# Norm factors from a matmul with ones, and the last up pair in seven products

## The chip, the cores and the metric

The kernel runs on one core of a Trainium2 chip. The metric is device time in microseconds of one launch; the number told for a kernel is the median of its runs. Engines are named as in the profile: PE is TensorE (matmuls; PEld its weight loads), DVE VectorE, ACT ScalarE, POOL GpSimd, SP the queue that issues most transfers.

## The reference

A two-layer encoder trunk over 512 positions with 1024 channels, in float32. Layer 0 mixes tokens with causal pooling and a short gated convolution, layer 1 with gated linear attention in 4 heads. After each mixer comes a gated feed-forward part with a convolution. Every part is preceded by an RMS norm, the attention output is normed per head, and a last norm ends the trunk.

```
def rmsnorm(x, g):
    y = x * rsqrt(mean(x * x, axis=-1) + EPS)
    return y * g

for l in range(2):
    hn = rmsnorm(x, mix_norm[l])
    if l == 0:
        y = concat(pool_mixer(...), sb * causal_dwconv(sc * sx)) @ ab_w_out
    else:
        y = gla_mixer(hn @ gla_w_in, ...) @ gla_w_out     # o * rsqrt(mean(o * o) + EPS) per head
    x = x + y
    u, v = split(rmsnorm(x, ffn_norm[l]) @ w_up[l])
    x = x + (gelu(causal_dwconv(u)) * v) @ w_down[l]
return rmsnorm(x, final_norm)
```

## The kernel before

Channels lie on the 128 partitions, the 512 positions along the free dimension, so x is 8 tiles of 128x512. Each matrix product is made of three matmul passes: both operands are split into a high and a low part (`split`, lines 157 to 159: ACT copies to a rounded type, DVE subtracts), and high by high, high by low and low by high are summed in one PSUM bank (`accumulate`, line 255; one output tile of 128 channels from 1024 takes 24 matmuls with 512 columns). Weights come from memory block by block through SP into three buffers `raw`; ACT makes `hi` (line 214), DVE makes `lo` (line 218).

The norm is applied late: the products are made of x times the gain, and the factor `rs`, one number per position, is multiplied in afterwards. ACT squares x (line 279) and DVE adds the squares into `acc`. `sums` (line 305) adds over the partitions with four matmuls that have `acc` as weights and one column of ones, so that positions lie on partitions (`ss`, 128x4). `rsqrt_small` (lines 282 to 292) takes the square root on ACT, the reciprocal on DVE, and one Newton step in three small DVE operations. `spread_small` (line 297) makes four matmuls with an identity to spread the 128x4 result over all partitions as 128x512 (`bc`), and ACT copies that to `rs` (line 319) or, per attention head, to `ro` (line 902). This happens at seven places with a wide result that the change touches: the first norm (`norm_rows`), the norm of each feed-forward part (`norm_parts`, in `ffn_up`) and the four heads (`out_norm`, `out_scale`). The norm ahead of the attention and the last one use the small form as well.

`ffn_up` makes 22 pairs of u and v tiles per layer. Pairs 1 to 20 use `seven`: u and v and the two halves of channels and positions are combined so that seven quarter products (each 12 matmuls with 256 columns, line 520) do the work of eight. Their weight sums need more transfers and work on ACT and DVE: `s31` is loaded by SP twice side by side and POOL's queue adds to it, the left half and a quarter are loaded, and three high and low parts and two differences are made (lines 471, 478, 483, 489). Pairs 0 and 21 use `plain`: v and u each with 24 matmuls of 512 columns (line 435). In this stage PE, DVE and ACT run in an order written out by hand: every step is entered with a due time by `at(...)`, in units of a product, and the list is sorted by it. The last products p4 and p3 of a pair are placed behind the first ones of the next pair. What follows on a pair (`keep` copies out of PSUM, line 528; the convolution, gelu, the product with v) ends in `ms[j]`, which `split_m` splits into `mh` and `ml` for the down product (`ffn_down`, PSUM tile `dn`). Eight side tiles share memory with the buffers of the seven-product stage: they hold `mh` and `ml` of the last four pairs.

Outside `ffn_up` the order on each engine is set by a scheduler from the program text: functions handed to `after(n, ...)` run n projections later (`tick`). In the attention stage, the four heads' scores, recurrences, outputs (`o`) and norms are so placed between the eight projections `r` (`gate_r`). `out_gate` of a head waits for `sil`, the silu of r, and then makes `y`, `yh` and `yl`. Each engine works through its own queue in order; a PE matmul that waits holds up all matmuls behind it.

Of the kernel before, what the change touches and what calls it, by code (L numbers as in the profile page):

```python
# [7 lines left out]
F32 = mybir.dt.float32  # L8
# [5 lines left out]
P = 128  # L14
# [27 lines left out]
UNIT = 1.364  # L42
PAIR = 7 * UNIT
PLAIN = 8 * UNIT
NORM = 1.6
PE_AT = {"p1": 0, "p2": 1, "p6": 3, "p5": 5, "p7": 6, "p4": 9, "p3": 11}
DOWN_K = (8, 7, 7)
DOWN_AT = (0, 8, 15)

# [14 lines left out]
def trunk_kernel(ctx, tc, xT, cols, w_ab, w_pool, w_abo, w_vg, w_qkr, w_g2, w_go, w_up, w_dn, outT):  # L64
# [11 lines left out]
    def slot(dt=F32, name="s"):  # L76
        return big.tile([P, T], dt, tag="s", name=name)
# [17 lines left out]
    def bank(name="ps"):  # L95
        return ps.tile([P, T], F32, tag="ps", name=name)
# [35 lines left out]
    for k in range(3, KD):  # L132
        x_load(k)

    cp.tile([P, 48], F32, tag="gap", name="gap")
# [4 lines left out]
    sp.tile([P, 72], F32, tag="gap", name="gap", bufs=1)  # L140
    warm_in = sp.tile([P, 1], F32, tag="warm", name="warm_in", bufs=1)
    S.activation(warm_in, ones[:, 0:1], AF.Sqrt)
# [4 lines left out]
    V.memset(eps_t, EPS)  # L147
    ident = cp.tile([P, P], F32, tag="ident", name="ident")
    G.memset(ident, 1.0)
    G.affine_select(ident, ident, [[-1, P]], ALU.is_equal, 0.0, base=0, channel_multiplier=1)  # L150
# [18 lines left out]
    def weight_order():  # L169
        for g in range(2, 4):  # L170
            yield w_ab[g], KD, P
        for j in range(4):
            for b in (8 + j, 12 + j, 4 + j):
                yield w_ab[b], KD, P
        for j in TILE_ORDER:
            yield w_abo[j], KD, P
        for l in range(2):
            for j in range(NF):
                if j in (0, NF - 1):
# [60 lines left out]
    def after(n, fn):  # L240
        pending.append((done[0] + n, fn))
# [40 lines left out]
    def rsqrt_small(dst, ssum, n, width):  # L282
        v = sp.tile([P, n], F32, tag=f"v{n}", name="v")
        V.tensor_scalar(v, ssum, 1.0 / width, EPS, ALU.mult, ALU.add)
        s = sp.tile([P, n], F32, tag=f"s{n}", name="s")
        S.activation(s, ssum, AF.Sqrt, bias=eps_t, scale=1.0 / width)
        y = sp.tile([P, n], F32, tag=f"y{n}", name="y")
        V.reciprocal(y, s)
        t = sp.tile([P, n], F32, tag=f"t{n}", name="t")
        V.tensor_tensor(t, y, v, ALU.mult)  # L290
        V.scalar_tensor_tensor(t, t, -0.5, y, ALU.mult, ALU.mult)
        return s, V.scalar_tensor_tensor(dst, t, 1.5, y, ALU.add, ALU.mult).ins

    def spread_small(y, n):
        b = bank("bc")[:, : n * P]
        for c in range(n):
            PE.matmul(
                b[:, c * P : (c + 1) * P], y[:, c : c + 1].broadcast_to([P, P]), ident, start=True, stop=True
            )
        return b  # L300

    def sums(acc, c0=0, n=NTT):
        b = bank("ss")
        for c in range(n):
            PE.matmul(b[:, c : c + 1], acc[:, (c0 + c) * P : (c0 + c + 1) * P], ones[:, 0:1], start=True, stop=True)
        return b

    def norm_parts(acc, gelu=False):
        y4 = sp.tile([P, NTT], F32, tag="y4", name="y4")
        rs = slot(name="rs")  # L310

        def one():
            s, last = rsqrt_small(y4, sums(acc)[:, :NTT], NTT, D)
            if gelu:
                S.activation(sp.tile([P, 1], F32, tag="warm", name="warm", bufs=1), s[:, 0:1], AF.Gelu)
            return last

        def two():
            S.activation(rs, spread_small(y4, NTT), AF.Copy)

        return y4, rs, one, two

    def norm_rows(acc, first, second):
        y4, rs, one, two = norm_parts(acc)
        after(first, one)
        after(second, two)
        return y4, rs

    def residual(j, o, next_gain, acc):
# [51 lines left out]
        return out  # L381

    def ffn_up(l, acc, mixed):
        _, rs, norm_one, norm_two = norm_parts(acc, True)
        skew = SKEW[l]
        lo_t, hi_t = slice(0, H), slice(H, T)
        k1, k2 = range(HK), range(HK, KD)
# [14 lines left out]
        def at(t, fn):  # L402
            events.append((t, len(events), fn))
# [44 lines left out]
        def seven(j, base):  # L448
# [96 lines left out]
            for name, out, first, ts in (  # L545
                ("p1", "x", True, lo_t), ("p2", "yz", True, lo_t), ("p6", "x", False, lo_t), ("p5", "yz", False, hi_t),
                ("p7", "x", False, lo_t), ("p4", "x", False, lo_t), ("p3", "yz", False, hi_t),
            ):
                at(base + PE_AT[name] * UNIT, lambda a=(name, out, first, ts): product(*a))
# [6 lines left out]
            at(after + 4.5, u_scaled)  # L556
            conv_at(j, after, q)
            at(after + 10.4, lambda: V.tensor_tensor(q["k"], b["yz"], q["k"], ALU.add))
            at(after + 12.3, lambda: V.tensor_tensor(q["a"], q["k"], q["a"], ALU.mult))

        mh, ml = [], []

        def split_m(n):
            for j in range(len(mh), min(len(mh) + n, NF)):
                make = side if j >= NF - NSIDE // 2 else slot
# [5 lines left out]
        at(2.5 * PLAIN / 6, norm_one)  # L571
        at(5.5 * PLAIN / 6 + NORM / 2, norm_two)
        step = PLAIN / 6
        base = PLAIN + NORM
        plain(0, 0.0, [i * step + NORM / 2 * ((i > 2) + (i > 5)) for i in range(6)], base)
        for j in range(1, NF - 1):
            seven(j, base)
            base += PAIR
        block(base - 14.0, base - 6.75, base - 4.35)
        block(base - 9.0, base - 2.7, base - 0.3)  # L580
        last = PLAIN + 2 * UNIT
        plain(NF - 1, base, [i * last / 6 for i in range(6)], base + last - 4.0)
        at(base + 2.0, lambda: open_stage("side"))
        for t in (0.6, 1.3, 2.0, 2.7, 5.7, 8.7, 9.4, 11.0):
            at(base + t, lambda: split_m(1))
        block(base - 3.0, base + 4.6, base + 9.0)
        with tc.manual_schedule(engines={mybir.EngineType.PE, mybir.EngineType.DVE, mybir.EngineType.Activation}):
            for t, _, fn in sorted(events, key=lambda e: e[:2]):
                fn()
# [55 lines left out]

    y_h = [slot(F32R, "yh") for _ in range(8)]
    y_l = [slot(F32R, "yl") for _ in range(8)]
    _, rs = norm_rows(acc, 1, 2)

    def pool_front(g, win, pu):  # L650
        u = slot(name="pu")
# [248 lines left out]
    def out_scale(h, ob, yo):  # L900
        ro = slot(name="ro")
        S.activation(ro, spread_small(yo, NTT), AF.Copy)
        ys = []
        for e in range(2):
            y = slot(name="y")
            V.scalar_tensor_tensor(y, ob[e], col("gnorm", e), ro, ALU.mult, ALU.mult)
            ys.append(y)
        after(1, lambda: out_gate(h, ys))
# [34 lines left out]
    tc.keep_in_program_order(S.activation(ready_in, ones[:, 0:1], AF.Sqrt))  # L943
    mixed = mix_out("go", "ffn1", acc)
    assert not pending

# [120 lines left out]
```

## Time and profile before

| | |
|---|---|
| median of 3 runs | 1045.44 us (1045.11 to 1045.96) |
| the profiled execution | 1045.42 us |
| its span from the first to the last instruction | 1043.7 us |
| busy share PE, PEld, DVE, ACT, POOL | 99, 89, 71, 54, 5% |
| mean granted TensorE clock | 0.997 |

The profile is one execution. A row of the timeline has the start, the duration from the first start to the last end, the engine, the line, the operation, output and inputs, and the count of instructions; in brackets stands the idle time before it and what ended that. Matmuls are pipelined, so the time one costs in a stream is the distance between starts and not its duration. A row of the list of waits has the total, the count and the longest wait. A matmul of plain 32-bit type shows as two records, one of the rounded type as one.

### The profile page before, as it was taken

Reading aid. Unit: us, or ns where it says so; the run is one execution under the profiler, and the core shown is the slowest. Engines: PE = TensorE matmul, PEld = TensorE weight load, DVE = VectorE, ACT = ScalarE, POOL = GpSimd, SP = SyncE. Lnnn points to the kernel's source line nnn. Section 1 sums busy time; section 2 is a strip of 40 time slices with the busy share of each in tenths; the row PEclk is TensorE's granted clock in tenths of the full one; section 3 lists DMA queues with packets and bytes.
Section 4 is the critical chain, followed back from the end, with each engine's and each line's share of the span. In section 5 each row is a group of like instructions: output and inputs, shape, how many; then the busy total and the mean of one; then the engine's idle time right before and its main releaser. Section 6 shows DMA issues by size and latency. Waiting matters only on the chain.

```text
span 1043.7 us, 16375 instructions
## 1 busy us (share of the span) xinstructions
PE 1030.1 (99%) x6614; PEld 929.2 (89%) x6614; DVE 739.9 (71%) x1060; ACT 560.0 (54%) x828; POOL 52.8 (5%) x79
## 2 busy tenths in 40 slices
PE   9999999999999999999999999999999999999996
PEld 7888889999999878889988888889999999988886
DVE  7875669999999874444465555678999999873333
ACT  6432557676667642234773355656766776653321
POOL 0001000110110000010000001000111110000000
PEclk9999999999999999999999999999999999999998
DMA  6436226878875243333232117135887775243312
GB/s 226 137 117 161 65 88 164 199 194 201 195 186 144 82 145 94 99 93 109 82 107 87 49 41 181 41 111 139 200 199 186 190 202 151 82 143 99 105 36 81
DMA packets 53644, 135.94 MB, mean 130 GB/s; under 512 B 4704, under 2 KB 7136, under 8 KB 53568
## 3 DMA queue, kind: packets, MB, share of 16 engines
q1 hardware_dynamic: 41456, 112.74, 34.2%
q0 software_dynamic: 10880, 20.97, 12.7%
q10 hardware_dynamic: 1232, 1.17, 0.4%
q8 instruction: 52, 0.85, 0.3%
q14 instruction: 24, 0.20, 0.1%
HBM read 132.77 MB, written 2.10 MB: 129 GB/s over the span
## 4 chain that ended last, share of the span: by engine, by line
PE 92%; DVE 3%; ACT 2%; DMA 1%; issue 1%; SPq 0%; DVEq 0%; ACTq 0%
PE dn L255 21%; PE stx L520 20%; PE styz L520 15%; PE r L255 4%; PE abo L255 4%; PE go L255 4%; PE q L255 2%; PE k L255 2%; PE pc L255 2%; PE px L255 2%; PE pb L255 2%; PE vg L804 1%; PE vg L802 1%; PE vg L803 1%; PE v L435 1%; PE u L435 1%
## 5 line engine op out<-in xcount | busy, mean ns | idle before, releaser
L214 ACT ACTIVATE hi<-raw 128x1024 fp32r<-128x1024 f32 (+3 forms) x111 | 112.9, 1019 | 164.8 <-PE dn L255 95.8
L218 DVE TENSOR_TENSOR lo<-raw,hi 128x1024 fp32r<-128x1024 f32 (+3 forms) x111 | 130.2, 1173 | 83.8 <-PE dn L255 48.5
L478 DVE TENSOR_TENSOR lo<-raw,hi 128x1024 fp32r<-128x1024 f32 x80 | 97.5, 1219 | 3.4 <-ACT hi L471 3.4
L471 ACT ACTIVATE hi<-raw 128x1024 fp32r<-128x1024 f32 x80 | 84.7, 1059 | 21.9 <-PE styz L520 17.2
L255 PE MATMUL dn<-mh,hi 128*128 128x512 f32 (+1 forms) x374 | 88.9, 377 | 0.5 <-ACT mh L158 0.5
L255 PE MATMUL dn<-mh,lo 128*128 128x512 f32 (+1 forms) x374 | 88.5, 376 | 0.0
L255 PE MATMUL dn<-ml,hi 128*128 128x512 f32 (+1 forms) x374 | 88.1, 376 | 0.0
L458 POOL DMA_DIRECT2D s<-in_w_up x40 | 48.2, 1205 | 670.8 <-DVE raw L489 189.6
L255 PEld LDWEIGHTS dn<-mh,hi 128*128 128x128 f32 x374 | 67.3, 188 | 14.6 <-ACT mh L158 1.9
L255 PEld LDWEIGHTS dn<-mh,lo 128*128 128x128 f32 x374 | 67.5, 188 | 12.9
L255 PEld LDWEIGHTS dn<-ml,hi 128*128 128x128 f32 x374 | 67.4, 188 | 12.8
L351 DVE SCALAR_TENSOR_TENSOR cacc<-u,colt,cacc 128x511 f32<-128x511 f32 x96 | 71.4, 744 | 2.4 <-ACT cacc L348 2.2
L348 ACT ACTIVATE cacc<-u,colt 128x512 f32<-128x512 f32 x48 | 39.2, 817 | 37.4 <-DVE u L543 29.4
L270 ACT ACTIVATE xh<-xall,colt 128x512 fp32r<-128x512 f32 x32 | 22.9, 723 | 58.4 <-DVE xall L330 57.0
L520 PE MATMUL stx<-th,hi 128*128 128x256 f32 x320 | 49.3, 276 | 0.0
L520 PE MATMUL styz<-xh,hi 128*128 128x256 f32 x320 | 49.3, 276 | 0.0
L520 PE MATMUL stx<-th,lo 128*128 128x256 f32 x320 | 49.3, 276 | 0.0
L520 PE MATMUL styz<-xh,lo 128*128 128x256 f32 x320 | 49.3, 276 | 0.0
L520 PE MATMUL styz<-xl,hi 128*128 128x256 f32 x320 | 49.3, 276 | 0.0
L520 PE MATMUL stx<-tl,hi 128*128 128x256 f32 x320 | 49.3, 276 | 0.0
L478 DVE TENSOR_TENSOR lo<-s,hi 128x1024 fp32r<-128x1024 f32 x40 | 48.6, 1216 | 0.0
L471 ACT ACTIVATE hi<-s 128x1024 fp32r<-128x1024 f32 x40 | 42.5, 1062 | 1.2
(279 smaller groups left out, 2304.3 us busy)
## 6 DMA issues: line engine op xcount, KB each, us to landing
raw<-in_w_up SPq DMA_DIRECT2D x48, 512.0 KB, 6.5
s<-in_w_up SPq DMA_DIRECT2D x40, 512.0 KB, 7.1
s<-in_w_up POOLq DMA_DIRECT2D x40, 512.0 KB, 6.5
raw<-in_w_dn SPq DMA_DIRECT2D x32, 448.0 KB, 3.2
raw<-in_w_up SPq DMA_DIRECT2D x40, 256.0 KB, 3.0
raw<-in_w_dn SPq DMA_DIRECT2D x16, 512.0 KB, 3.5
raw<-in_w_qkr SPq DMA_DIRECT2D x16, 512.0 KB, 3.6
raw<-in_w_ab SPq DMA_DIRECT2D x14, 512.0 KB, 3.5
```

The costliest lines, as they stand in the source:

```text
L214: S.activation(parts[0], raw, AF.Copy)
L218: V.tensor_tensor(parts[1], raw, f32(parts[0]), ALU.subtract)
L255: PE.matmul(out, w[:, k, :], a[k], start=first and i == 0 and k == 0, stop=last and i == 2 and k == n - 1)
L270: done = S.activation(xh[k], x[k], AF.Copy, scale=col(gname, k))
L348: S.activation(acc[0], u, AF.Identity, bias=col(bname, j), scale=col(wname, 2 * nj + j))
L351: V.scalar_tensor_tensor(a, u[:, : T - i], col(wname, (2 - i) * nj + j), a, ALU.mult, ALU.add)
L435: PE.matmul(o, w[:, k, :], a[k], start=i == 0 and k == 0, stop=i == 2 and k == KD - 1)
L458: G.dma_start(w["s31"].rearrange("p (a n) -> p a n", a=2), src, accum_op=ALU.add)
L471: S.activation(h, src(), AF.Copy)
L478: V.tensor_tensor(lo, src(), f32(h), ALU.subtract)
L520: PE.matmul(b[out][:, ts], wt[:, ks[k]], a[k], start=first and i == 0 and k == 0, stop=i == 2 and k == HK - 1, skip_group_check=True,)
L802: PE.matmul(o[c][:, :n], xh[kk][:, cs], h[:, k, :], start=kk == 0, stop=False)
```

## The change

1. `norm_wide` replaces the small form at the seven places. It splits `acc` into `nh` (ACT) and `nl` (DVE), sums over partitions with two matmuls whose weights are a 128x128 tile of ones, so that every partition gets the sums 512 wide, takes the inverse root from a table on ACT (`ny`), and makes one Newton step in four wide operations (square on ACT, DVE, ACT, DVE) to `rs`. The first norm makes `nh` and `nl` at once and the rest one projection later; `ffn_up` enters the eight parts by due times; `out_norm` runs all of them in a row, and `out_scale` follows one projection later.
2. In the small form that remains, the root and the reciprocal become one inverse root on ACT.
3. In `ffn_up` the load of the gelu table is an entry of its own, behind the norm; the two waits of 0.8 units that were left for the norm become one of 0.46.
4. Pair 21 is made by `seven`. Its p3 goes ahead of p4 and into a bank of its own (`stw`), which one more DVE addition brings to `kk`. The due times of the last down blocks and of the `mh`, `ml` splits move, and the side tiles now hold `mh` and `ml` of the first four pairs.
5. Two unused gap tiles shrink.

```
+    def norm_wide(acc, width, name="rs"):
+        ah, al = slot(F32R, "nh"), slot(F32R, "nl")
+        y, t, rs = slot(name="ny"), slot(name="nt"), slot(name=name)
...
+        def totals():
+            b.append(bank("ss"))
+            PE.matmul(b[0], ones_r, ah, start=True, stop=False)
+            PE.matmul(b[0], ones_r, al, start=False, stop=True)
+        return rs, (
+            lambda: S.activation(ah, acc, AF.Copy),
+            lambda: V.tensor_tensor(al, acc, f32(ah), ALU.subtract),
+            totals,
+            lambda: S.activation(y, b[0], AF.Abs_reciprocal_sqrt, bias=eps_t, scale=1.0 / width),
+            lambda: S.activation(t, y, AF.Square),
+            lambda: V.scalar_tensor_tensor(t, b[0], width * EPS, t, ALU.add, ALU.mult),
+            lambda: S.activation(t, t, AF.Identity, bias=half3, scale=-0.5 / width),
+            lambda: V.tensor_tensor(rs, t, y, ALU.mult),
+        )
...
     def out_norm(h, ob, sq):
-        yo = sp.tile([P, NTT], F32, tag="yo", name="yo")
-        rsqrt_small(yo, sums(sq)[:, :NTT], NTT, 256)
-        after(1, lambda: out_scale(h, ob, yo))
+        ro, norm = norm_wide(sq, 256, "ro")
+        for step in norm:
+            step()
+        after(1, lambda: out_scale(h, ob, ro))
...
+        for t, part in zip((4.0, 4.8, 4.9 * step, 9.6, 10.3, 11.2, 11.9, 12.6), norm):
+            at(t, part)
+        at(12.0, gelu_table)
...
-        for j in range(1, NF - 1):
+        for j in range(1, NF):
             seven(j, base)
             base += PAIR
-        block(base - 14.0, base - 6.75, base - 4.35)
-        block(base - 9.0, base - 2.7, base - 0.3)
-        last = PLAIN + 2 * UNIT
-        plain(NF - 1, base, [i * last / 6 for i in range(6)], base + last - 4.0)
-        at(base + 2.0, lambda: open_stage("side"))
-        for t in (0.6, 1.3, 2.0, 2.7, 5.7, 8.7, 9.4, 11.0):
+        base -= PAIR
+        block(base - 3.0, base + 4.4, base + 5.2)
+        at(base + 5.6, lambda: open_stage("side"))
+        for t in (5.8, 7.0, 8.8, 9.3, 10.6, 11.1, 12.5, 13.2):
             at(base + t, lambda: split_m(1))
-        block(base - 3.0, base + 4.6, base + 9.0)
...
+PE_AT_LAST = {"p1": 0, "p2": 1, "p6": 3, "p5": 5, "p7": 6, "p3": 7, "p4": 8}
```

More of the change, by code (lines that the diff above doesn't have):

```diff
@@ L133, in trunk_kernel @@
         x_load(k)
-    cp.tile([P, 48], F32, tag="gap", name="gap")
+    cp.tile([P, 40], F32, tag="gap", name="gap")
     ones = cp.tile([P, P], F32, tag="ones", name="ones")
@@ L139, in trunk_kernel @@
     V.tensor_copy(ones_r, ones)
-    sp.tile([P, 72], F32, tag="gap", name="gap", bufs=1)
+    sp.tile([P, 56], F32, tag="gap", name="gap", bufs=1)
     warm_in = sp.tile([P, 1], F32, tag="warm", name="warm_in", bufs=1)
-    S.activation(warm_in, ones[:, 0:1], AF.Sqrt)
+    S.activation(warm_in, ones[:, 0:1], AF.Abs_reciprocal_sqrt)
     warm = ps.tile([P, T], F32, tag="ps", name="warm")
@@ L284, in rsqrt_small @@
         V.tensor_scalar(v, ssum, 1.0 / width, EPS, ALU.mult, ALU.add)
-        s = sp.tile([P, n], F32, tag=f"s{n}", name="s")
-        S.activation(s, ssum, AF.Sqrt, bias=eps_t, scale=1.0 / width)
         y = sp.tile([P, n], F32, tag=f"y{n}", name="y")
-        V.reciprocal(y, s)
+        S.activation(y, ssum, AF.Abs_reciprocal_sqrt, bias=eps_t, scale=1.0 / width)
         t = sp.tile([P, n], F32, tag=f"t{n}", name="t")
@@ L306, in sums, with norm_rows @@
         return b
-    def norm_parts(acc, gelu=False):
+    def norm_rows(acc, first, second):
         y4 = sp.tile([P, NTT], F32, tag="y4", name="y4")
         rs = slot(name="rs")
[L312 to L326, printed above, removed]
+        after(first, lambda: rsqrt_small(y4, sums(acc)[:, :NTT], NTT, D))
+        after(second, lambda: S.activation(rs, spread_small(y4, NTT), AF.Copy))
         return y4, rs
@@ L383, in ffn_up @@
     def ffn_up(l, acc, mixed):
-        _, rs, norm_one, norm_two = norm_parts(acc, True)
+        rs, norm = norm_wide(acc, D)
         skew = SKEW[l]
@@ L548, in seven @@
             ):
-                at(base + PE_AT[name] * UNIT, lambda a=(name, out, first, ts): product(*a))
+                if j == NF - 1 and name == "p3":
+                    out, first = "w", True
+                when = PE_AT_LAST if j == NF - 1 else PE_AT
+                at(base + when[name] * UNIT, lambda a=(name, out, first, ts): product(*a))
             at(base + 1.45, keep_p1)
@@ L647, in trunk_kernel, with first_norm @@
     y_l = [slot(F32R, "yl") for _ in range(8)]
-    _, rs = norm_rows(acc, 1, 2)
+    rs, norm = norm_wide(acc, D)
+    for step in norm[:2]:
+        step()
+    def first_norm():
+        for step in norm[2:]:
+            step()
+    after(1, first_norm)
     def pool_front(g, win, pu):
```

28 lines of the change are left out of this document (17 added, 11 removed).

## The prediction

> **What bounds the kernel now.** I read the page's busy shares first, then what TensorE (PE) waited for, then the timeline of each place that the change touches.
>
> ```profile
> span 1043.7 us, 16375 instructions
> PE 1030.1 (99%) x6614; PEld 929.2 (89%) x6614; DVE 739.9 (71%) x1060; ACT 560.0 (54%) x828; POOL 52.8 (5%) x79
> PE stx L520 <- ACT kk L528: 2.5, 2, 1.3
> ```
>
> PE is busy 99% of the span; the largest entry in its list of waits is 2.5 us, two waits at the start of the up stages. So PE's own instructions set the time, and a matmul taken away is worth its full interval, unless PE is then made to wait. A busy duration overlaps its neighbour; what counts is the distance between starts:
>
> ```profile
> 344.42 0.62 PE L520 MATMUL stx<-th,hi 128*128 128x256 f32 x4
> 344.87 0.62 PE L520 MATMUL stx<-tl,hi 128*128 128x256 f32 x4
> 345.78 2.00 PE L435 MATMUL v<-xh,hi 128*128 128x512 f32 x8
> 347.62 1.97 PE L435 MATMUL v<-xl,hi 128*128 128x512 f32 x8
> ```
>
> Four 256-wide matmuls take 0.455 us (0.1135 each), eight 512-wide ones about 1.82 (0.227 each).
>
> **The change part by part: last up pair.** 48 wide matmuls (10.9) become 84 narrow ones (9.53): -1.36 per layer. On POOL one accumulating load is added, on SP the two 512 KB loads become a 512, a 512 and a 256 KB one. They follow the rhythm of 20 earlier pairs per layer, issued 15 to 26 us ahead, and I cost them at nothing.
>
> ```profile
> s<-in_w_up POOLq DMA_DIRECT2D x40, 512.0 KB, 6.5
> 372.61 1.54 PE L255 MATMUL dn<-mh,hi 128*128 128x512 f32 x5 [0.26 <-ACT mh L158]
> 373.65 0.19 PEld L255 LDWEIGHTS dn<-mh,hi 128*128 128x128 f32 x1 [0.27 <-ACT mh L158]
> 351.45 2.00 ACT L214 ACTIVATE hi<-raw 128x1024 fp32r<-128x1024 f32 x2
> 162.25 0.82 ACT L348 ACTIVATE cacc<-u,colt 128x512 f32<-128x512 f32 x1 [0.67 <-DVE u L362]
> ```
>
> But the splits of m (mh on ACT and ml on DVE, 0.62 and 0.68 like the yh and yl quoted below) barely keep up today: PE waited 0.26 and 0.27 there, about 0.7 by the distances between its starts. Now ACT and DVE also do the seven-product sums, and the splits start later. Following the new order from the pair's start at 345.78: ACT takes the copy of u (waits for p4 of the pair before, 350.1), hi of the first down block, cacc, mh0, a keep, mh1, hi (to 354.5), gelu (waits for DVE's second tap, 355.3), mh2, hi, mh3 (to 357.9). PE reaches the fourth down matmul after eight products and three matmuls, 345.78+10.9+0.7=357.3, and waits 0.6. On DVE ml7 ends at 364.0, PE wants it at 363.7; ml14 is 0.4 late. New waits 1.4, old ones 0.7: the pair nets -0.7 per layer, **-1.4**. Ends: no wait left, -4.0; one 1.2 us lo more in the queue at each place, +1.
>
> **First norm.** Four 1-wide fp32 sums and four 128-wide spreads become two wide matmuls.
>
> ```profile
> 24.13 0.95 PE L305 MATMUL ss<-ones,acc 128*128 128x1 f32 x8
> 24.94 2.11 PE L255 MATMUL pu<-xh,hi 128*128 128x512 f32 x8
> 30.53 1.05 PE L297 MATMUL bc<-ident,y 128*128 128x128 f32 x8
> 31.33 2.09 PE L255 MATMUL pc<-xh,hi 128*128 128x512 f32 x8
> 32.25 0.69 DVE L652 TENSOR_TENSOR pu<-pu,rs 128x512 f32<-128x512 f32 x1 [0.24 <-ACT rs L319]
> 37.05 0.50 PE L670 MATMUL po<-ph,pwh 128*128 128x512 f32 x1
> ```
>
> 0.81+0.80 become 0.45: PE would be 1.2 ahead. But po hangs on rs. In the new order rs comes behind ny, two weight copies and the Newton parts on ACT, and behind two weight lo's on DVE; then one more lo stands ahead of pu, which starts at 31.8 (now 32.25). So **-0.4**; ends 0 and -1.2.
>
> **Start of each up stage.** bc (0.80) goes, ss shrinks by 0.36, so PE comes to p6 earlier; p6 waits for the copy kk of p1.
>
> ```profile
> 150.68 1.28 ACT L315 ACT_TABLE_LOAD   x1
> 151.97 0.20 ACT L315 ACTIVATE warm<-s 128x1 f32<-128x1 f32 x1
> 158.79 0.62 PE L520 MATMUL styz<-xh,lo 128*128 128x256 f32 x4
> 160.26 0.36 ACT L528 ACTIVATE kk<-stx 128x256 f32<-128x256 f32 x1
> 160.68 0.53 PEld L520 LDWEIGHTS stx<-th,sh 128*128 128x128 f32 x4 [1.48 <-ACT kk L528]
> ```
>
> New: ss ends at 153.4, ACT then does ny (0.7, my estimate between a plain 512-wide copy's 0.6 and the 0.82 of cacc, which has a pointer for scale and one for bias), sh (0.6), square (0.6), a weight copy that waits for DVE (to 157.1), the Newton line (0.7), table load (1.28), warm, kk: to 159.5. PE arrives at 157.8, so its wait lengthens to 1.7, yet p6 starts 1.15 earlier; the next keep gives 0.2 back. **-1.0 per layer, -2.0**. Ends: -4.6 with the whole wait gone, +0.4 if the load drains. The Trainium skill ("ScalarE: Activation LUTs", What ACT_TABLE_LOAD costs) gives 1283 ns plus a drain of about 1380 ns per switch; by that kk would be 1.4 later and the sum +0.4 per layer. The rows show 1.28 and the next ACTIVATE 0.01 later, so I take no drain.
>
> **The four head norms.**
>
> ```profile
> 581.69 0.95 PE L305 MATMUL ss<-ones,osq 128*128 128x1 f32 x8
> 582.49 1.11 PE L870 MATMUL kv<-vt,kt 128*128 128x256 f32 x4
> 589.42 1.05 PE L297 MATMUL bc<-ident,yo 128*128 128x128 f32 x8
> 590.31 0.61 PE L884 MATMUL o<-att,vt 128*128 128x128 f32 x4
> 601.75 0.95 PE L305 MATMUL ss<-ones,osq 128*128 128x1 f32 x8
> 601.95 0.69 DVE L921 TENSOR_TENSOR r<-r,rs 128x512 f32<-128x512 f32 x1 [3.05 <-PE r L255]
> 602.55 0.68 DVE L159 TENSOR_TENSOR yl<-y,yh 128x512 fp32r<-128x512 f32 x1
> 602.67 0.63 ACT L922 ACTIVATE r<-r 128x512 f32<-128x512 f32 x1 [0.91 <-DVE r L921]
> 603.33 0.69 DVE L915 TENSOR_TENSOR y<-y,r 128x512 f32<-128x512 f32 x1
> 604.77 0.62 ACT L158 ACTIVATE yh<-y 128x512 fp32r<-128x512 f32 x1
> 606.87 1.21 DVE L218 TENSOR_TENSOR lo<-raw,hi 128x1024 fp32r<-128x1024 f32 x1
> 591.50 1.41 DVE L906 SCALAR_TENSOR_TENSOR y<-o,colt,ro 128x512 f32<-128x512 f32 x2
> ```
>
> Per head 0.80+0.89 become 0.45: -1.24, four times -5.0. Against it stands a new wait. Today ss reads osq, which DVE had long before. Now it reads nh (ACT) and nl (DVE), and where those stand in the queues decides. For the first head nh comes before PE is done with k: no wait. For the second and third, the order of the changed kernel puts nh on ACT behind silu of r and behind the second yh, and PE has ss right after that same r projection. From the end of r, today's 601.75: DVE r*rs starts 0.2 later (0.6 to the next), yl 0.6, a weight lo 1.14, y*r 0.68 to +3.2; ACT yh 0.63, nh 0.62 to +4.4; ss begins at +4.5 instead of 0. nl stands behind another yl and ends at +5.2, so the second ss waits 0.5 more: **5.0 us of idle PE, twice**, with kv and the scores (or the outputs) of other heads queued behind ss. For the fourth head nh stands behind silu alone: r*rs to +0.9, silu to +1.55, nh to +2.1: 2.15 of wait; five r matmuls run; nl is behind two y (1.41), lo and y*r, ends at +4.6, and PE waits 1.1 more. One kv waits 0.2 for st. Sum 13.4. The head norms net -5.0+13.4 = **+8.4**. Ends: without yl and lo in the way 1.7 less at each of the two, +5; with another lo there, +11.
>
> **Other parts.** The reciprocal leaves the last chain, from which the outputs hang:
>
> ```profile
> 1035.97 0.17 DVE L288 RECIPROCAL y<-s 128x2 f32<-128x2 f32 x1 [0.33 <-ACT s L286]
> 1036.17 0.16 DVE L290 TENSOR_TENSOR t<-y,v 128x2 f32<-128x2 f32 x1
> ```
>
> **-0.2**. The norm ahead of the gated attention keeps its small form; its reciprocal is hidden under the vg matmuls. Memset and gap tiles cost nothing on PE.
>
> Sum: -1.4-0.4-2.0+8.4-0.2 = +4.4 on 1045.42 us of the profiled execution (span 1043.7 and 1.7 around it; the median of the runs is 1045.44): 1049.8.
>
> **The clock.** PE has so far hardly paused. Where it did, at the end:
>
> ```profile
> 1034.53:1037.94 3.41, 1.54 (x10) 1.26 (x10) 1.22 (x6) 0.29 (x2) 0.00 (x0) 1.00 0.17 60
> 157.90:161.30 3.40, 2.12 (x19) 1.92 (x18) 3.37 (x4) 2.00 (x3) 0.00 (x0) 1.00 0.17 58
> 1037.90:1043.70 5.80, 0.00 (x0) 0.00 (x0) 2.29 (x5) 0.00 (x0) 0.00 (x0) 0.50 0.53 181
> ```
>
> (Columns: stretch, length, busy PE, PEld, DVE, ACT, POOL, granted clock, DMA share, GB/s.) A stretch of 3.4 us with PE 45% busy by tiny matmuls was followed by half clock; one with 62% was not. A pause of 4.5 us leaves one such stretch under 40% wherever it falls. I estimate the clock halves near its end and for about 3.2 us after it, half of which is lost: 1.6 per pause, 3.2 for the two long ones (ends 0, and 5.0 with the fourth head's too). I take the fall for both, since these pauses are emptier than the stretch that made it fall: 1049.8+3.2 = **1053.0**. The Trainium skill ("TensorE: Matmul & The Clock Gate", The HAM clock gate) says that one idle window of about 3.4 us throttles to half, and that windows run freely; by a window that must be wholly idle a 4.5 us pause would be hit about one time in three, and the time would mostly be the first rival's.
>
> **Rivals.** First: the pauses come but the clock holds: 1049.8. For it speaks that the last stretch's matmuls were small ones, so nothing proves that 40% of full ones is too little. Second, on the other side: the pauses don't come, because nh and nl are made before their r ends; then the heads give -5.0 and the sum is -1.4-0.4-2.0-5.0-0.2 = -9.0: 1036.4. It decides where ACT takes nh: before silu of the same r, faster; behind it, slower. Against it speaks the written order of ACT, and row 602.67, where silu waits for DVE and all behind it too. Third: the pauses are half as long, since yl and lo are out of the way and the fourth head doesn't wait; 13.4 becomes about 8, sum -1.0, clock mostly held: 1044.4, no measurable change. That the table root might need table loads of its own I leave out: the changed kernel's order has as many loads as before, and none between ny and the two lines behind it. Fourth: the tails wait longer than worked out, by 1 to 2 each: 1055 to 1057.
>
> **How the numbers follow.** Pauses with a fallen clock 0.53 (1051 to 1055), pauses with the clock held 0.25 (1048 to 1051), longer tails 0.10, half pauses 0.06, no pauses 0.06. The likeliest gives 1053.0. The range leaves out the last two and half of the fourth: 1047.5 to 1056.5. About 0.2% (2.1 us) is what a measurement can tell from no change. Faster 0.06; same 0.06; slower 0.88.
>
> **What the changed profile would show.** In the list of PE's waits: ss for nh and nl, two of about 4.5 us and one of 2; a granted clock under 1.00 between the second head's norm and the go projection; p6 waiting 1.7 for kk; short waits of dn for mh and ml after each up stage; no bc rows but those of the small norms. If ss does not wait in the heads, I am wrong in sign; if it waits and the clock stays at 1.00, in size by 3.

## Result and the profile after

The changed kernel took 1061.38 us (median of 4 runs, 1057.38 to 1065.07) against 1045.61 us for the kernel before in the same comparison (1045.11 to 1045.96): a ratio of 1.015 (95% interval 1.0112 to 1.0189). It is 15.8 us slower. The prediction said 1053.0, and 1047.5 to 1056.5 for the range. The profiled execution took 1060.2, with a span of 1058.5. The page of the changed kernel begins so (the last line is the granted clock in 40 slices):

```profile
span 1058.5 us, 16360 instructions
PE 1030.6 (97%) x6588; PEld 926.1 (87%) x6588; DVE 755.5 (71%) x1058; ACT 576.7 (54%) x854; POOL 55.6 (5%) x81
PEclk9999999999999999999999988999999999999998
```

PE's own busy time hardly moved (1030.1 before), its share fell from 99% to 97%, and the granted clock has a dent in two slices that the kernel before does not have. What PE waited for, longest sums first (us in total, times, longest):

```profile
PE ss L302 <- ACT nh L306: 10.6, 3, 4.3
PE stx L528 <- ACT kk L536: 3.4, 2, 1.7
PE po L695 <- ACT ph L161: 1.4, 1, 1.4
...
PE dn L258 <- ACT mh L161: 0.8, 2, 0.4
...
PE ss L303 <- DVE nl L307: 0.5, 1, 0.5
```

From PE's timeline of the changed kernel, the sums of the second, third and fourth head:

```profile
603.85 0.79 PE L302 MATMUL ss<-nh,ones_r 128*128 128x512 f32 x1 [4.30 <-ACT nh L306]
...
633.01 0.79 PE L302 MATMUL ss<-nh,ones_r 128*128 128x512 f32 x1 [4.30 <-ACT nh L306]
...
646.60 0.50 PE L302 MATMUL ss<-nh,ones_r 128*128 128x512 f32 x1 [1.97 <-ACT nh L306]
...
649.08 0.80 PE L303 MATMUL ss<-nl,ones_r 128*128 128x512 f32 x1 [0.52 <-DVE nl L307]
```

Around each of the three standstills the granted clock falls. Stretches of the changed kernel, in pairs: the 3.41 us ahead of a fall, then the fall (columns: stretch, length, busy PE, PEld, DVE, ACT, POOL with counts, granted clock, DMA share, GB/s):

```profile
599.95:603.36 3.41, 0.00 (x0) 0.00 (x0) 2.71 (x5) 1.35 (x3) 0.00 (x0) 1.00 0.21 19
603.36:613.60 10.24, 9.74 (x30) 7.10 (x31) 3.27 (x6) 4.51 (x7) 0.00 (x0) 0.50 0.11 45
627.26:630.67 3.41, 1.45 (x7) 0.87 (x5) 1.92 (x3) 1.89 (x3) 0.00 (x0) 1.00 0.00 0
630.67:637.49 6.82, 4.46 (x17) 3.86 (x18) 3.09 (x5) 4.47 (x6) 0.00 (x0) 0.50 0.20 77
644.31:647.72 3.41, 1.45 (x7) 0.96 (x6) 3.04 (x4) 3.22 (x4) 1.21 (x1) 1.00 0.64 186
647.72:654.56 6.84, 6.32 (x16) 4.49 (x15) 1.99 (x4) 1.45 (x3) 2.41 (x2) 0.50 1.02 188
```

At half clock PE did 9.74 + 4.46 + 6.32 = 20.5 us of work; half of that, 10.3 us, is lost.

Where the 14.8 us between the two spans (1058.5 and 1043.7) lie follows from the starts of the same instructions in both traces: front until the first v +0.2; v to p6 in the two layers -0.87 and -0.88; p6 to the last down product -0.34 and -0.27; ahead of the first r -0.4; from the first r to the first go product +17.0 (68.3 before, 85.4 after); end +0.3. So all of the loss lies in the 85 us of the r projections and the heads: 11.1 of waiting, less some 4.3 for the shorter norm matmuls there (the run that prices the half clock, below, gives this number), leaves 10.2 for the clock, and the busy time at half clock gives 10.3.

### The profile page after: what moved, and what is told of

Read it like the earlier page. It is cut to its first block, busy times and chain, and to the rows that moved or that the text cites. A ratio compares the mean times of both kernels' runs of the same rounds, so it can differ in the third digit from the quotient of the medians.

```text
span 1058.5 us, 16360 instructions
## 1 busy us (share of the span) xinstructions
PE 1030.6 (97%) x6588; PEld 926.1 (87%) x6588; DVE 755.5 (71%) x1058; ACT 576.7 (54%) x854; POOL 55.6 (5%) x81
## 5 line engine op out<-in xcount | busy, mean ns | idle before, releaser
L217 ACT ACTIVATE hi<-raw 128x1024 fp32r<-128x1024 f32 (+3 forms) x107 | 108.8, 1017 | 161.2 <-PE dn L258 94.4
L221 DVE TENSOR_TENSOR lo<-raw,hi 128x1024 fp32r<-128x1024 f32 (+3 forms) x107 | 125.4, 1172 | 83.8 <-PE dn L258 48.8
L486 DVE TENSOR_TENSOR lo<-raw,hi 128x1024 fp32r<-128x1024 f32 x84 | 102.4, 1220 | 0.4 <-ACT hi L479 0.4
L479 ACT ACTIVATE hi<-raw 128x1024 fp32r<-128x1024 f32 x84 | 89.0, 1059 | 24.5 <-PE styz L528 16.6
L466 POOL DMA_DIRECT2D s<-in_w_up x42 | 50.6, 1205 | 700.2 <-ACT hi L217 174.6
L258 PEld LDWEIGHTS dn<-mh,lo 128*128 128x128 f32 x374 | 67.5, 188 | 12.8
L528 PE MATMUL stx<-th,hi 128*128 128x256 f32 x336 | 52.1, 277 | 0.0
L528 PE MATMUL stx<-tl,hi 128*128 128x256 f32 x336 | 51.8, 276 | 0.0
L528 PE MATMUL stx<-th,lo 128*128 128x256 f32 x336 | 51.7, 276 | 0.0
L486 DVE TENSOR_TENSOR lo<-s,hi 128x1024 fp32r<-128x1024 f32 x42 | 51.1, 1217 | 0.0
```

What stands on the lines that cost most here:

```text
L217: S.activation(parts[0], raw, AF.Copy)
L221: V.tensor_tensor(parts[1], raw, f32(parts[0]), ALU.subtract)
L258: PE.matmul(out, w[:, k, :], a[k], start=first and i == 0 and k == 0, stop=last and i == 2 and k == n - 1)
L466: G.dma_start(w["s31"].rearrange("p (a n) -> p a n", a=2), src, accum_op=ALU.add)
L479: S.activation(h, src(), AF.Copy)
L486: V.tensor_tensor(lo, src(), f32(h), ALU.subtract)
```

## Experiments

Theory: nh and nl come late because of their place in the queues of ACT and DVE, and the standstills that follow lower the clock. The first three runs take the lateness, the wide head norms, and the empty PE away, one at a time. "The stages" below are the starts of the same instructions, as above.

**Early nh and nl.**

```
 in outputs(), behind the add of osq:
+    ro, norm = norm_wide(sq, 256, "ro")
+    for step in norm[:2]: step()
+    after(1, lambda: out_norm(h, ob, ro, norm[2:]))
```

> Changed kernel, with the head norms' nh and nl issued one step earlier, right behind the add that makes osq; nothing is left out. Theory (PE stands still because nh and nl are queued behind silu and yh, and the half clock follows from the standstill): no wait of ss for nh above 0.5 us, clock 1.00 through the gated attention; against the kernel before -5.0 for the shorter head norms and -1.9 for what the other parts give by the starts of the stages in the two profiles (+0.2 at the front, -1.3 and -1.1 in the two feed-forward layers, +0.3 at the end): 1038.5. Rival A (ACT and DVE are too full, and the earlier nh only makes kt, osq or r late instead): as much waiting elsewhere, 1050 to 1060. Rival B (the low clock has another cause than the standstill): waits gone, clock still under 1.00, about 1048.

Measured: 1047.03 (10 runs, 1043.0 to 1048.6), ratio 1.0011 (0.9999 to 1.0024). The clock stayed at 1.00, and from the first r to go the kernel took 67.5 us instead of 85.4: theory right on the place and the mechanism. One wait of 2.6 us is left, in the fourth head, whose osq is itself late. But the sum missed by 8.5, and only 2.6 of that is this wait. Most of the rest is in a place where nothing had been changed: from p6 to the last down product the first layer took 324.1 us, 5.4 more than in the changed kernel's profile. Matmuls of PE in the same 170 us of the two up stages, early nh and nl:

```profile
170.00:340.00 170.00, 170.00 (x1459) 170.00 (x1459) 156.93 (x210) 114.55 (x175) 20.41 (x17) 1.00 0.76 190
720.00:890.00 170.00, 170.00 (x1502) 170.00 (x1501) 161.44 (x216) 117.65 (x181) 21.66 (x18) 1.00 0.76 193
```

PE is never idle and the clock is 1.00 in both, but in the first stage it starts 1459 matmuls and not 1502: 116.7 ns from start to start, not 113.3. The changed kernel's profile has the quick pace in both stages (1502 in the first).

**Head norms in their old form, the rest of the change kept.**

```
-    ro, norm = norm_wide(sq, 256, "ro")
+    yo = sp.tile([P, NTT], F32, tag="yo", name="yo")
+    rsqrt_small(yo, sums(sq)[:, :NTT], NTT, 256)
 ... out_scale: ro from spread_small(yo, NTT), as before
```

> Changed kernel with the four head norms in their old form (1-wide sums, four spreads); nothing is left out. Theory (all of the loss lies in the head norms): no half clock, and the rest of the change by itself: 1041.4 by the terms of the prediction (-4.0), 1043.5 by the starts of the stages in the two profiles (-1.9). Rival (part of the loss lies in the front, the up stages or the tails): 1045.4 or more.

Measured: 1047.28 (10 runs, 1046.58 to 1047.94), ratio 1.0019 (1.0009 to 1.0029). No wait in the heads and no half clock; r to go as before the change (68.35). It missed the sum too, and again by pace: 1491 and 1490 matmuls in the two stretches above. Here it is single products, in every pair those with the sh and sl weights, 0.47 us for four instead of 0.455:

```profile
253.56 0.62 PE L528 MATMUL stx<-tl,hi 128*128 128x256 f32 x4
254.01 0.62 PE L528 MATMUL stx<-th,lo 128*128 128x256 f32 x4
254.47 0.63 PE L528 MATMUL stx<-th,sh 128*128 128x256 f32 x4
254.94 0.63 PE L528 MATMUL stx<-tl,sh 128*128 128x256 f32 x4
255.41 0.63 PE L528 MATMUL stx<-th,sl 128*128 128x256 f32 x4
```

**Idle work for PE in the pauses.**

```
+    for _ in range(fill): PE.matmul(b[0], ones_r, xh[0], start=True, stop=True)
     PE.matmul(b[0], ones_r, ah, start=True, stop=False)      # fill = (0, 18, 18, 8)[h]
```

> Changed kernel with idle work for PE: ahead of the ss sums of the second and third head 18, of the fourth head 8 matmuls of 512 columns whose result is overwritten by ss; nothing is left out. They take about 0.227 each, so PE comes to ss as late as nh does (the 4.3 us wait becomes 4.1 of matmuls and 0.2 of waiting), and its stream is never empty. Theory (half clock follows from the standstill and costs about 10: 9.75, 4.5 and 6.3 us of busy time at half clock, half of it lost): clock 1.00 and 1060.2 - 10.2 = about 1050. By the size that the prediction gave to the clock (3.2): 1057. Rival (clock falls whatever PE does, or the long stretch has another cause): 1060.

Measured: 1053.46 (4 runs, 1052.54 to 1054.14), ratio 1.0079 (1.0064 to 1.0094). From the first r to go 74.0 us at a clock of 1.00 instead of 85.4. The total stands higher than expected because this run, too, had the slow pace in its first up stage (1460 matmuls). So the low clock comes from the standstill and costs about 10, but the price had to be measured again without the slow pace.

**Where do the slow paces come from?** First rival: the place of the tiles, which the new small tiles moved. The side and up tiles began at byte 204160 of a partition before, 203904 after the change, and 203968 in the run with old head norms. The next three runs move them to 204160 with the gap tile.

```
-    sp.tile([P, 56], F32, tag="gap", name="gap", bufs=1)
+    sp.tile([P, 120], F32, tag="gap", name="gap", bufs=1)     # 104 with the old head norms
```

> The run with early nh and nl, and the gap tile in the sp pool 120 instead of 56 floats wide, so that the up stage's tiles and the side tiles start 256 bytes higher, at byte 204160 of a partition as in the kernel before (203904 in the changed kernel). Nothing is left out. In the run with early nh and nl the first up stage took 205.1 us from its first p2 to its first down product, 5.5 more than in the changed kernel's profile: every 256-wide matmul started 116.7 ns after the one before it instead of 113.3, although the clock was 1.00. Theory 1 (the place of the tiles lets PE fall into this slower pace): pace 113.3 in both up stages and 1040.5, which is the sum of the stages with the up stage at 199.5. Theory 2 (the pace is fixed by chance at the last wait ahead of it, wherever the tiles lie): still 1043 to 1048, one up stage or the other at 116.7.

> The run with head norms in their old form, and the gap tile in the sp pool 104 instead of 56 floats wide, so that the up stage's tiles start at byte 204160 as in the kernel before (203968 in the run without this, which is no multiple of 128). Nothing is left out. In that run the products with the sh weights took 0.47 instead of 0.455 us per four matmuls in every pair, and the down products 231 to 237 ns per matmul instead of 227. Theory 1 (the place of the tiles costs this): both gone, and the rest of the change alone gives 1043.2 by the stages (front -0.2, each feed-forward layer about -1.1, end +0.2). Theory 2 (the pace is chance): about 1047 again.

> The changed kernel with the gap tile in the sp pool 120 instead of 56 floats wide, so that the up stage's tiles start at byte 204160 as in the kernel before; nothing is left out. The four runs of the changed kernel spread from 1057.4 to 1065.1; the profiled one (1060.2) had both up stages at 113.3 ns per matmul. Theory 1 (place of the tiles): the slow runs go, 1057 to 1061, median about 1059, and what is left over the kernel before is waits and half clock in the head norms. Theory 2 (chance): the same spread as the changed kernel, median about 1061.

Measured: early nh and nl 1048.2 (10 runs, 1046.1 to 1048.85), ratio 1.0025 (1.0016 to 1.0035), 1460 matmuls again; old head norms 1047.77 (10 runs, 1042.43 to 1048.58), ratio 1.0013 (0.9998 to 1.0028); changed kernel 1061.5 (4 runs, 1059.22 to 1063.54), ratio 1.0153 (1.0132 to 1.0175). So the place explains the slow sh products alone: they are gone from the profile of old head norms (1503 matmuls). It does not explain the 116.7 ns. The ten runs with old head norms fall in two groups, three at 1042.4 to 1043.4 and seven at 1047.7 to 1048.6, some 5 us apart with nothing between: chance.

The profile of early nh and nl with moved tiles shows at which instruction the pace changes. PE, and ACT at the same time:

```profile
159.83 0.74 PE L528 MATMUL stx<-th,sh 128*128 128x256 f32 x4 [1.70 <-ACT kk L536]
...
162.23 0.62 PE L528 MATMUL styz<-th,lo 128*128 128x256 f32 x4
162.76 0.73 PE L528 MATMUL stx<-th,hi 128*128 128x256 f32 x4
163.33 0.63 PE L528 MATMUL stx<-tl,hi 128*128 128x256 f32 x4
163.80 0.63 PE L528 MATMUL stx<-th,lo 128*128 128x256 f32 x4
```

```profile
161.62 0.82 ACT L356 ACTIVATE cacc<-u,colt 128x512 f32<-128x512 f32 x1 [0.90 <-DVE u L370]
162.34 0.37 ACT L536 ACTIVATE kk<-stx 128x256 f32<-128x256 f32 x1
```

From 162.23 to 162.76 is 0.53 instead of 0.45: p7 waits some 0.07 for the second kk copy, which stands behind cacc on ACT. Behind this second wait four matmuls take 0.47, until the next wait two hundred us later. In the changed kernel's profile it was the other way round: the wait at the same place, at 162.90 and some 0.02 long, ended a slow pace that had begun at the first one:

```profile
161.47 0.63 PE L528 MATMUL styz<-th,hi 128*128 128x256 f32 x4
161.94 0.63 PE L528 MATMUL styz<-tl,hi 128*128 128x256 f32 x4
...
163.94 0.62 PE L528 MATMUL stx<-th,lo 128*128 128x256 f32 x4
164.39 0.62 PE L528 MATMUL stx<-xh,hi 128*128 128x256 f32 x4
```

Second rival, then: a short wait close behind the long one can leave PE's stream in either pace, which it keeps until it next stops. It is tried from both sides: taking the second wait away, and giving one to the kernel before.

```
-    at(base + 6.05, lambda: keep(q["k"][:, hi_t]))
+    at(base + (5.1 if j == 1 else 6.05), lambda: keep(q["k"][:, hi_t]))
```

> The run with early nh and nl and the up stage's tiles placed as before, and in addition the second kk copy of each layer's first seven-product pair put on ACT ahead of cacc instead of behind it; nothing is left out. In the run without this PE stood a second time at the start of the up stage, about 0.07 us, in front of p7, and from there to the end of the stage its 256-wide matmuls came every 116.7 ns instead of every 113.3 (5.6 us in all). Theory 1 (this second wait starts the slow pace): no second wait, pace 113.3 in both layers, 1040.5 in every run. Theory 2 (any wait can start it, the first and longer one too): most runs 1040 to 1041, some 1046 to 1048. Theory 3 (the pace has to do with neither): median 1048 again.

> The run with head norms in their old form and the tiles placed as before, and in addition the second kk copy ahead of cacc; nothing is left out. It gives the rest of the change by itself. Without the copy moved, three of ten runs took 1042.4 to 1043.4 and seven 1047.7 to 1048.6. Theory 1 (second wait starts the slow pace): all runs 1042.5 to 1043.5, that is -2.2 against the kernel before (the prediction's terms gave -4.0). Theory 2 (any wait): most at 1043, some at 1048. Theory 3: as without.

> The changed kernel with nothing but the second kk copy put ahead of cacc; nothing is left out. Theory 1: the slow pace goes, and what is left is the head norms: waits and half clock, 1057 to 1060.5 and median about 1058.5; the spread that stays is that of the half clock. Theory 2 or 3: 1057 to 1065, median about 1061.

```
 kernel before:
+    for _ in range(2 if j == 1 else 1):
         at(base + 6.05, lambda: keep(q["k"][:, hi_t]))
```

> The kernel before, with the second kk copy of each layer's first seven-product pair made twice, so that PE has to wait a second time at the start of the up stage, some 0.3 us; nothing is left out. Theory 1 (a second wait just behind the first can start the slow pace of 116.7 ns for the rest of the stage, in any kernel): 1045.2 + 0.6 = 1045.8 where it doesn't start, 1051 or so where it does in one layer, and runs of both kinds. Theory 2 (the slow pace comes from something else that the change brought): 1045.4 to 1046.2 in all runs.

Measured without the second wait: early nh and nl 1042.19 (7 runs, 1040.31 to 1044.73), ratio 0.9971 (0.9958 to 0.9983); old head norms 1042.19 (7 runs, 1041.7 to 1042.41), ratio 0.9971 (0.996 to 0.9982); the changed kernel 1058.78 (4 runs, 1057.54 to 1060.17), ratio 1.0131 (1.0116 to 1.0146). With old head norms the group at 1048 is gone, and all three profiles have 1502 or 1503 matmuls in the first stage. With early nh and nl the runs still spread over 4 us; the standstill of 2.6 in the fourth head is left there, and the clock explains the spread. The profiled run, 1041.7, has a fall behind that standstill:

```profile
627.98:631.39 3.41, 0.77 (x4) 0.35 (x3) 2.14 (x4) 2.15 (x5) 0.42 (x1) 1.00 0.87 256
631.39:634.80 3.41, 3.41 (x9) 2.65 (x9) 2.89 (x5) 3.33 (x4) 2.86 (x3) 0.50 0.73 141
```

Of the seven runs, the two at 1040.3 and 1040.5 have a mean granted clock of 0.997, the five from 1041.7 to 1044.7 one of 0.994 to 0.996. In the two earlier profiles of early nh and nl the clock held behind the same standstill.

Measured with a second wait in the kernel before: 1051.29 (4 runs: 1046.69, 1051.19, 1051.39, 1051.46), ratio 1.0045 (1.0028 to 1.0063). Its profile, in which p7 waits 0.26:

```profile
162.60 0.62 PE L520 MATMUL styz<-th,lo 128*128 128x256 f32 x4
163.32 0.73 PE L520 MATMUL stx<-th,hi 128*128 128x256 f32 x4
163.89 0.63 PE L520 MATMUL stx<-tl,hi 128*128 128x256 f32 x4
164.35 0.63 PE L520 MATMUL stx<-th,lo 128*128 128x256 f32 x4
```

```profile
170.00:340.00 170.00, 170.00 (x1459) 170.00 (x1459) 157.03 (x209) 114.60 (x174) 19.21 (x16) 1.00 0.73 184
720.00:890.00 170.00, 169.90 (x1499) 169.71 (x1498) 161.59 (x216) 118.24 (x181) 20.46 (x17) 1.00 0.76 188
```

The same wait in both layers, the slow pace in one. So a second wait is enough for it, in a kernel that has nothing else of the change, and by chance. Why PE's stream has these two paces stays open: no row shows what it lacks in the slow one.

**The price of the half clock, without the slow pace.** The changed kernel with the copy moved and the idle matmuls:

> The changed kernel with the second kk copy put ahead of cacc (1058.8 in the run with that alone) and the idle matmuls ahead of ss in the second, third and fourth head, so that PE's stream isn't empty there. Nothing is left out. It prices the half clock without the slow pace in the way. Theory (three falls cost about 10): 1058.8 - 10 = 1049, every run within 1. By the prediction's size (3.2): 1055.6.

Measured: 1047.55 (10 runs, 1046.47 to 1048.83), ratio 1.0015 (1.0004 to 1.0026). Against 1058.78 with the pauses empty: 11.2 us. The waits for nh and nl are gone from its list. The 44 idle matmuls in their place take 10.0 us, 1.1 less than the waits took in the changed kernel's profile, so about 10 of the 11.2 are the clock. From r to go the kernel takes 74 us at full clock; without the 10.0 that is 64.0, 4.3 less than before the change:

```profile
580.80:654.80 74.00, 74.00 (x381) 61.93 (x380) 43.88 (x72) 38.32 (x54) 3.61 (x3) 1.00 0.38 93
```

**Wide head norms where there is time for them.** Three, three with one late, and two, on top of the run with old head norms and the copy moved:

```
+    if h == HEADS - 1:                  # two wide: if h > 1
         after(1, lambda: out_norm(h, ob, sq))     # old form
+        return
+    ro, norm = norm_wide(sq, 256, "ro")           # nh and nl here, the rest a step later
     # one late: nh and nl of h == 1 a step later too
```

> The run with head norms in their old form and the second kk copy moved, and in addition the first three heads' norms in the wide form with nh and nl made early; only the fourth head keeps the old form. Nothing is left out. Theory (a wide head norm saves its 1.24 us wherever nh and nl are made in time, and the fourth head has no time): no wait of ss for nh, clock 1.00, 1042.2 - 3.7 = 1038.5. Rival (early nh and nl push back other work of the heads by as much): 1041 to 1043.

> The run with three wide head norms, but in the second head nh and nl are issued as late as in the changed kernel, so that PE stands once, 4.3 us. Nothing is left out. By the prediction's size of the clock (1.6 per long standstill): 1038.5 + 4.3 + 1.6 = 1044.4. By the changed kernel's profile, where a fall lasted two or three stretches of 3.41 us: 1038.5 + 4.3 + 2.5 to 5 = 1045.3 to 1047.8, differing from run to run. If one standstill doesn't lower the clock: 1042.8.

> The run with the old form in all four head norms and the second kk copy moved (1042.2), and in addition the first two heads' norms in the wide form with nh and nl made early. Nothing is left out. Theory (a wide norm saves 1.24 until PE comes to the fourth head's ss ahead of the osq add, which it did by 2.0 us with three wide norms): PE comes 2.5 earlier than with none, a wait of at most 0.8 for osq is left, 1040.5. Rival (early nh and nl cost elsewhere what they save): 1042 or more.

Measured: three 1042.69 (9 runs, 1041.86 to 1044.89), ratio 0.9978 (0.9968 to 0.9987); one late 1051.49 (4 runs, 1049.61 to 1052.92), ratio 1.0062 (1.0047 to 1.0078); two 1041.05 (5 runs, 1040.89 to 1041.31), ratio 0.9959 (0.9945 to 0.9973). With three, PE comes to the fourth head's sum before its data:

```profile
631.01 1.05 PE L327 MATMUL ss<-ones,osq 128*128 128x1 f32 x8 [1.98 <-DVE osq L917]
```

What the third wide norm saves, and more, is spent there, and the expected 1038.5 was missed by 4.2. The clock has a part in it too, since the five runs from 1042.7 to 1044.9 have a mean granted clock of 0.994 or 0.995 and the four shorter ones 0.996 or 0.997. With two this wait is gone. One late pair of nh and nl costs 8.8 us between the medians, twice its 4.3 of waiting. In the profile of one late, the stretch around its standstill:

```profile
595.00:601.40 6.40, 4.45 (x20) 3.36 (x18) 5.70 (x12) 2.21 (x3) 0.00 (x0) 1.00 0.29 82
601.40:608.30 6.90, 4.54 (x12) 2.89 (x12) 3.09 (x5) 4.55 (x7) 0.00 (x0) 0.51 0.28 76
```

Not all of the 8.8 belongs to this standstill: the same profile has a second fall, 3.41 us at half clock from 639.03 on, behind the fourth head's wait for osq, where the profile of three wide has none.

The run with two wide norms is the best version found: by its ratio 4.3 us below the kernel before, and 20 below the changed kernel.

## Why the prediction was right and wrong

**The step that failed is the size of the clock term.** "I estimate the clock halves near its end and for about 3.2 us after it, half of which is lost: 1.6 per pause, 3.2 for the two long ones", with 0 and 5.0 as its ends. The mechanism was right: the clock does halve around each pause, 0.5 us before the end of the first, 2.3 before the end of the second and 1.1 behind the end of the third. But it stays down for 10.2, 6.8 and 6.8 us, it also falls behind the fourth head's pause of 2 us, which I had only in the upper end, and it costs 10.3 by the profile and about 10 by the run with idle matmuls. Even the upper end was less than half of it. In the profiled execution this is nearly the whole miss: 10.3 less 3.2 is 7.1, and 1060.2 less 1053.0 is 7.2. I took the one fall that the profile of before shows, at its very end, as if the clock came back one stretch later; that row had no work behind it from which a return could be read.

The Trainium skill ("TensorE: Matmul & The Clock Gate", The HAM clock gate) gives windows of 3413 ns and full clock only after a busy one. The falls here are three, two and two times 3.41 us, and their starts lie 8 and 5 times 3.41 us apart. The stretch in which PE starts again was busy for 2.91, 1.05 and 2.90 of the 3.41 us, and a whole busy one had to follow; in the first fall even the middle stretch, fully busy with matmuls 64 wide, did not end it. Of the twelve falls ahead of the end in all the profiles, the five whose first stretch was 88% busy or more lasted 3.4 us, and the seven with 85% or less lasted 6.8 to 13.7. The three longest have stretches of mostly 64-wide matmuls behind the first one; that such matmuls count for less is not shown.

The Trainium skill's other rule there, that a window without work lowers the clock, is too narrow for this trace: ahead of the second and third fall PE was busy 1.45 of 3.41 us. My reading that a stretch under 40% is enough held, and the profiles together give the limit. Cut into stretches of 3.41 us that begin where the falls begin, the 16 profiles have 28 falls, the ones at the end included. Each follows a stretch in which PE was busy 46% of the time or less, and none of the stretches with 47% or more is followed by one. The nearest from above, in the profile of the changed kernel with moved tiles, has 1.60 of 3.41 us and full clock behind it; the fall came only after the emptier stretch:

```profile
628.42:631.83 3.41, 1.60 (x8) 0.98 (x6) 1.77 (x3) 2.04 (x3) 0.00 (x0) 1.00 0.00 0
631.83:635.24 3.41, 0.60 (x2) 0.29 (x2) 2.55 (x4) 2.10 (x3) 0.00 (x0) 1.00 0.46 141
```

So a pause of 4.3 us always made a fall here, and for one of 2 us it depends on how it lies in these stretches: the fourth head's left 42% in the changed kernel's profile, and 49% without a fall in the profile with the copy moved.

**The head norms** came nearly as told: the shorter matmuls gave 4.7 of the 5.0 (4.3 from r to go and 0.4 ahead of r), and ss waits for nh behind yh and silu. In ACT's rows of the second head, silu is the one that makes r:

```profile
600.31 0.63 ACT L946 ACTIVATE r<-r 128x512 f32<-128x512 f32 x1 [0.96 <-DVE r L945]
602.64 0.63 ACT L161 ACTIVATE yh<-y 128x512 fp32r<-128x512 f32 x1 [1.71 <-DVE y L939]
603.18 0.61 ACT L306 ACTIVATE nh<-osq 128x512 fp32r<-128x512 f32 x1
```

Two waits of 4.3 (told 5.0, of which the 0.5 for nl did not come), and 2.0 + 0.5 in the fourth (told 3.2): 11.1 instead of 13.4, net +6.4 instead of +8.4.

**Up-stage starts.** p6 waits 1.70 (told 1.7), and starts 0.87 earlier after v (told 1.15). The upper end of this term should have been +0.8, twice the +0.4 that the prediction names per layer; it made no difference, since the table load did not delay kk by a drain, in the changed kernel's ACT rows:

```profile
158.15 1.28 ACT L591 ACT_TABLE_LOAD   x1
159.44 0.20 ACT L591 ACTIVATE warm<-ones_r 128x1 f32<-128x1 f32 x1
159.55 0.36 ACT L536 ACTIVATE kk<-stx 128x256 f32<-128x256 f32 x1
```

"The next keep gives 0.2 back" was some 0.02 and 0.1 in the two layers, so -0.8 per layer. But that small wait, priced at its own length, is what can throw the stage into the slow pace. Moving the copy brought the changed kernel's median from 1061.4 to 1058.8, a part of the miss in no term of mine. How large a part is not settled, since the intervals of the two ratios overlap. That the slow pace struck some of the four runs is likely: the two longest, 1062.6 and 1065.1, have about the same mean granted clock (0.989 and 0.987) as the two shorter (0.989 and 0.985), so the clock does not explain their length. The profiled run had hardly any of it, and 1058.8 still lies above the range.

**Last pair.** -0.34 and -0.27 from p6 to the last down product, with that small wait in it: about -0.4 in each instead of -0.7. The wait worked out as 0.6 for the fourth down matmul stands in PE's timeline with two thirds of that:

```profile
357.42 0.50 PE L258 MATMUL dn<-mh,hi 128*128 128x512 f32 x1 [0.41 <-ACT mh L161]
```

**First norm and last chain.** The -0.4 of the first norm was +0.2 in the profile, just past its upper end: po waited 1.4 for ph, more than the 1.2 that PE was ahead. In the other profiles with this front v starts anywhere from 142.5 to 143.8 (one with a fall of the clock there aside), against 143.5 and 143.0 with the old one: too little to tell. The -0.2 of the last chain did not show: the end was 0.3 longer here and 0.1 to 0.2 shorter in some of the runs.

**The sum** without the clock was +4.4. The profile gives 14.8 less 10.3, +4.5. That was luck, since misses on both sides cancelled: 2.3 less waiting in the heads, 2.4 less gain in all the rest. The second rival (no pauses, 1036.4) was the one that an edit could reach, by making nh and nl early, but not to that figure: the best version took 1041.05. Two of the four norms had to keep the old form there, and the parts outside the heads, in the run with all four old and the copy moved, gave 3.0 by its ratio where my terms say 4.0.

## What to carry to other kernels

Where an engine runs its queue in order, a new short instruction saves nothing until its operands are made ahead of the work it would stand behind; see in the written order what stands ahead of each operand, and issue the operand where its input is born. Price a standstill of the matmul engine at its length plus the clock that follows: in this kernel 11.1 us of waiting in four places cost another 10. Count the matmuls per stretch when a stage is longer and the engine is still 100% busy: busy time and clock say nothing there, and the count showed a pace 3% lower.

## What the hardware did that was not expected

PE's stream of 256-wide matmuls has two steady paces at the same clock, 113.3 and 116.7 ns. A wait can leave it in either, and it keeps that until its next wait, 200 us later. That cost 5.4 us in the profile of early nh and nl, and is about the distance between the two groups of runs. A wait of 0.07 us is enough. One of 15 runs of the kernel before, in the last comparison, took 1050.9 against 1044.7 to 1046.5 for the others, about what one slow stage costs; it was not profiled, so that it was this is not shown.

The place of a tile counts: with the side and up tiles starting 64 bytes past a multiple of 128, the products with the sh and sl weights took 3% longer or more, and moving the tiles by 192 bytes removed it, in all five profiles with that place.

The clock falls behind short pauses too. In the profile of the changed kernel with moved tiles, po's wait of 1.9 us in the front was enough (the wait, and the fall behind it):

```profile
34.50:37.90 3.40, 1.47 (x7) 0.93 (x6) 3.37 (x7) 2.06 (x5) 0.00 (x0) 1.00 0.36 135
37.90:41.30 3.40, 3.40 (x9) 2.68 (x9) 3.33 (x8) 0.64 (x3) 0.00 (x0) 0.50 0.50 154
```
